# RWKV output scaling from GpSimd to VectorE, with three of the planner's waits made longer

## The chip, the cores and the metric

The kernel runs on one core of one Trainium2 chip. The metric is the device time of one execution in microseconds, the median of several runs. In the profile PE is TensorE (matmuls), PEld its weight loads, DVE is VectorE, ACT is ScalarE, POOL is GpSimd and SP is SyncE, which here issues most of the DMAs. Each engine works through its own queue of instructions in order.

## The reference

A decoder trunk of two layers over one sequence of 1024 tokens, width 1024, all in f32. The first (even) layer runs RWKV-7 time mixing with 16 heads of 64, an S5 state space model and cross-attention to a memory of 256 tokens behind one input projection and one output projection; the second (odd) layer has Mamba-2, latent attention and memory attention in the same layout. The part that matters here is the group norm at the end of the RWKV branch: the outputs `y` of each head and token are centred, scaled and shifted before a bonus is added.

```python
y = seq_major(y).astype(jnp.float32)
mean = jnp.mean(y, -1, keepdims=True)
var = jnp.mean(jnp.square(y - mean), -1, keepdims=True)
y = ((y - mean) * lax.rsqrt(var + RW_GN_EPS)).astype(p.dtype).reshape(b, s, h * n) * ln_w + ln_b
bonus = jnp.sum(r * k * r_k, -1, keepdims=True) * v
return y + bonus.reshape(b, s, h * n)
```

The result is multiplied by a SiLU gate cut from the same input projection.

## The kernel before, in words

Projections are "dense" items: a tile of 128 output columns for two halves of 512 tokens, each half 24 matmuls (8 blocks of the contraction, each in three products of high and low parts), which line 179 issues. They form one long list (`dense`), the lowest in rank: the RWKV projections, then two for the memory's queries, gates, the S5 inputs, the first four S5 gates `zs`, and then an item that waits for `mem`, an event at the start of the S5 stage. Gates are evacuated by ScalarE and by VectorE's line 418.

The RWKV branch is cut into 16 units, each a pair of heads and half of the tokens. For each unit several streams run:

- A (`rw_prep0`) prepares keys and decay. It waits `BK` before the matmuls of the head sums and `HA` before the half products, whose result `ga` ScalarE copies at line 653.
- V (`rw_inv0`) inverts 32x32 triangular blocks: `ga` goes out by DMA (`d_in`), comes back spread over the partitions (`ai`), is worked by 62 small POOL instructions (lines 710 and 712), and goes out and in once more (`d_out`, `xt`). VectorE then transposes small blocks (line 727) for the matmuls of `rw_inv1` (stream I).
- B (`rw_prep1`) makes transposed copies and masks.
- S (`rw_seq`) runs four blocks of 128 tokens one behind the other, and leaves the outputs in a PSUM bank `yps`.
- O (`rw_out`) does the group norm: VectorE sums and centres (lines 841 to 844), ScalarE squares, VectorE sums again (line 848) and finds the reciprocal root with three Newton steps (`rsqrt`, lines 869 to 877) on a 128x8 tile `gmv`; POOL multiplies the 128x512 tile by it (line 850); TensorE transposes the product (line 183); VectorE applies weight and shift, bonus and gate (lines 858 to 862), and SP stores it.

The order of TensorE's instructions is fixed by a planner (`Flow`) when the program is made. It walks through planned microseconds: a stream yields what it waits for (an event, a free PSUM bank, or a number of planned microseconds), and at each step the stream of lowest rank that is ready goes on. A matmul of 512 columns counts 512 / 2400 planned us. A wait in it costs no time on the chip by itself; it decides what TensorE does in between. The tile framework orders the other engines' instructions with a timeline of its own.

The events tie the streams: A of unit n waits for B of unit n-1, B of unit n for A of unit n and S of unit n-2, S of unit n for I and B of unit n. V's due time is made in `stream_a`, from `pool_t[0] = max(pool_t[0], F.now + 10) + HV` and `F.done(("V", n), pool_t[0] + HW - F.now)`, with `HV = 16` and `HW = 14`.

After the last unit the RWKV pools are closed and the S5 stage opens: VectorE and POOL build its parameters, and TensorE begins with transposes of the tile `rn`.

Of the kernel before, what the change touches and what calls it, by code (L numbers as in the profile page):

```python
# [14 lines left out]
A = mybir.AluOpType  # L15
# [109 lines left out]

H = 2.0
HZ = 1.2
HA = 12
HV = 16
S5A = 10  # L130
S5B = 30
HW = 14

S5Q = 12
S5P = 6
MX = 9
MY = 5
ML = 4
BK = 6.5
BL = 1  # L140
S5M = 13
S5Y = 10
# [122 lines left out]
class K:  # L265
# [303 lines left out]
    def rw_prep0(self, st, p, lat, l2, k, wk):  # L569
# [9 lines left out]
        parts = self.pp_parts(sq)  # L579
        yield [BK, ("g", 1)]  # L580
        ps = self.bank("g")
# [44 lines left out]
        ga = wk.tile([P, 4, 2, P], F32, name="ga", bufs=2)  # L626
        yield [HA, ("g", 2)]
        self.half_products(bm, kr, 0, ga)
# [205 lines left out]
    def rw_out(self, p, hh, st, zd, wk):  # L834

        nc, F = self.nc, self.flow
        s = slice(hh * HT, (hh + 1) * HT)
        yp = st["yp"].rearrange("p b (h i) -> p (b h) i", h=2)
        b8 = lambda ap: ap.unsqueeze(2).broadcast_to([P, 8, 64])
        mv = wk.tile([P, 4, 8], F32, name="gmv", bufs=1)  # L840
        nc.vector.tensor_reduce(mv[:, 0], yp, AX.X, A.add)
        nc.vector.tensor_scalar(mv[:, 0], mv[:, 0], 1.0 / 64, None, A.mult)
        y = wk.tile([P, 8, 64], F32, name="ty", bufs=1)
        nc.vector.tensor_tensor(y, yp, b8(mv[:, 0]), A.subtract)
        F.rel("yps", 3.0)
        sq = wk.tile([P, 8, 64], F32, name="sz", bufs=1)
        nc.scalar.square(sq, y)
        nc.vector.tensor_reduce(mv[:, 1], sq, AX.X, A.add)
        self.rsqrt(mv[:, 1], mv[:, 1], mv[:, 2:4], 1.0 / 64, 64e-5)
        nc.gpsimd.tensor_tensor(y, y, b8(mv[:, 1]), A.mult)  # L850
        sz = wk.tile([P, HT], F32, name="sz", bufs=1)
        nc.sync.dma_start(sz, zd[p, :, s])
        yield [10.0, ("g", 1)]
        tp = self.bank("g", (P, 4, P))
        for b in range(4):
            F.transpose(tp[:, b, :], y[:, 2 * b:2 * b + 2].rearrange("p h i -> p (h i)"), self.ident)
        o = wk.tile([P, HT], F32, name="ty", bufs=1)
        nc.vector.tensor_scalar(o, tp.rearrange("p b t -> p (b t)"), self.col("rw_ln_w", p), self.col("rw_ln_b", p),
                                A.mult, A.add)
        F.rel("g", 1.2)  # L860
        nc.vector.tensor_tensor(o, o, st["bon"], A.add)
        nc.vector.scalar_tensor_tensor(o, o, 0.5, sz, A.mult, A.mult)
        self.put_y(p, s, o)
# [49 lines left out]
    def rw_streams(self, cp, wk, rd, zd, npairs=8):  # L913
# [38 lines left out]
        def stream_a():  # L952
            yield "lat"
            lt = latents()
            for n, (p, h) in enumerate(units):
# [8 lines left out]
                pool_t[0] = max(pool_t[0], F.now + 10) + HV  # L964
                F.done(("V", n), pool_t[0] + HW - F.now)

# [1503 lines left out]
```

## Time and profile before

| what | value |
|---|---|
| median of 3 runs | 2760.64 us (2759.63 to 2765.98) |
| the profiled execution's own time | 2757.28 us |
| its span, first to last instruction | 2755.3 us |
| mean granted TensorE clock | 0.954 |
| busy: PE, DVE, ACT, POOL | 2522.3, 1785.2, 1250.2, 804.7 us |

In the rows a line such as `L850 POOL TENSOR_TENSOR ty<-ty,gmv` names the line of the kernel, the engine, the operation and the tiles it writes and reads; `mm` and `g` are PSUM banks. A row of a timeline begins with its start and its length in us, and a bracket at its end tells how long the engine was idle before it and what ended that. A row of stretches gives the stretch, its length, each engine's busy time with the count of its instructions, the granted share of TensorE's clock (1.0 is 2.4 GHz, 0.5 is 1.2 GHz), the share of the DMA engines and GB/s.

### The profile page before, as it was taken

What the parts mean: (1) busy time and instruction counts of PE and PEld (TensorE: products, weight loads), DVE (VectorE), ACT (ScalarE), POOL (GpSimd) and SP (SyncE); (2) the same over time, 40 slices, a digit from 0 to 9 for tenths busy, and PEclk for the clock granted to TensorE, in tenths of its full rate; (3) what the DMA queues carried; (4) which work ended last, traced back from release to release, by engine and by line L of the source; (5) the groups of instructions that cost most, each with busy time, mean ns of one, the idle gap of its engine ahead of it and who ended that gap; (6) DMA issues with size and microseconds to landing.
All of it is one profiled execution on the core that took longest, in us unless ns stands there. A gap on an engine that the chain in (4) does not pass through costs nothing. (4 is left out here: it accounts for less than half of the span.)

```text
span 2755.3 us, 42347 instructions
## 1 busy us (share of the span) xinstructions
PE 2522.3 (92%) x15058; PEld 2036.7 (74%) x15058; DVE 1785.2 (65%) x3366; ACT 1250.2 (45%) x2446; POOL 804.7 (29%) x1507
## 2 busy tenths in 40 slices
PE   7998899999999998888999998988999979998997
PEld 5776677777777776666688776767778768887786
DVE  8756656665755537788656446786743887777532
ACT  7443334443443333545543346435443546655443
POOL 3533554355435403254200111252312020000011
PEclk9999999999999999987999999999999999999999
DMA  4432232333332243355584554142344431113543
GB/s 147 131 100 78 83 94 89 98 89 94 89 100 73 72 133 137 109 151 180 158 280 142 159 183 142 62 108 91 101 144 162 161 117 56 57 50 123 189 133 101
DMA packets 263859, 328.27 MB, mean 119 GB/s; under 512 B 88016, under 2 KB 135248, under 8 KB 263136
## 3 DMA queue, kind: packets, MB, share of 16 engines
q1 hardware_dynamic: 260736, 319.39, 37.6%
q0 software_dynamic: 1280, 4.20, 0.5%
q8 instruction: 119, 1.95, 0.3%
q10 hardware_dynamic: 1632, 1.98, 0.2%
q14 instruction: 92, 0.75, 0.1%
HBM read 232.59 MB, written 92.90 MB: 118 GB/s over the span
## 5 line engine op out<-in xcount | busy, mean ns | idle before, releaser
L405 DVE TENSOR_TENSOR wl<-w,wh 128x512 fp32r<-128x512 f32 (+2 forms) x410 | 287.4, 705 | 282.2 <-ACT wh L404 271.5
L404 ACT CAST wh<-w 128x512 fp32r<-128x512 f32 (+2 forms) x410 | 241.9, 594 | 410.8 <-PE mm L179 259.4
L179 PE MATMUL mm<-xhi,wh 128*128 128x512 f32 x832 | 366.1, 440 | 30.0 <-DVE ev L418 18.5
L179 PE MATMUL mm<-xlo,wh 128*128 128x512 f32 x832 | 341.7, 411 | 4.5 <-DVE xlo L496 2.4
L179 PE MATMUL mm<-xhi,wl 128*128 128x512 f32 x832 | 340.3, 409 | 0.0
L179 PE MATMUL mm<-x1h,wh 128*128 128x512 f32 (+1 forms) x608 | 253.3, 417 | 25.2 <-ACT craw L1818 14.2
L179 PE MATMUL mm<-x1l,wh 128*128 128x512 f32 (+1 forms) x608 | 241.9, 398 | 0.0
L179 PE MATMUL mm<-x1h,wl 128*128 128x512 f32 (+1 forms) x608 | 241.7, 397 | 0.0
L710 POOL TENSOR_TENSOR titmp<-ai,ti 128x60 f32<-128x60 f32 (+24 forms) x496 | 153.1, 309 | 296.5 <-DMA ai<-d_in 259.9
L179 PEld LDWEIGHTS mm<-xhi,wh 128*128 128x128 f32 x832 | 163.9, 197 | 84.6 <-DVE ev L418 20.2
L179 PEld LDWEIGHTS mm<-xhi,wl 128*128 128x128 f32 x832 | 163.8, 197 | 39.7
L179 PEld LDWEIGHTS mm<-xlo,wh 128*128 128x128 f32 x832 | 164.5, 198 | 36.6 <-DVE xlo L474 5.3
L712 POOL TENSOR_TENSOR ti<-ti,titmp 128x60 f32<-128x60 f32 (+24 forms) x496 | 161.3, 325 | 38.2
L179 PEld LDWEIGHTS mm<-x1h,wh 128*128 128x128 f32 (+1 forms) x608 | 117.0, 192 | 59.1 <-ACT craw L1818 17.7
L179 PEld LDWEIGHTS mm<-x1l,wh 128*128 128x128 f32 (+1 forms) x608 | 117.1, 193 | 27.0 <-issue 3.6
L179 PEld LDWEIGHTS mm<-x1h,wl 128*128 128x128 f32 (+1 forms) x608 | 116.6, 192 | 26.8 <-DVE wl L405 0.2
L179 PE MATMUL mm<-yb,wh 128*128 128x512 f32 x320 | 103.6, 405 | 4.3 <-ACT yb L404 4.0
L799 ACT ACTIVATE sn<-s0c,fin 64x64 f32<-64x64 f32 x128 | 44.1, 345 | 104.3 <-DVE s0c L827 57.6
L785 DVE TENSOR_TENSOR gb<-g,m 128x256 f32<-128x256 f32 x128 | 49.4, 417 | 64.3 <-PE g L179 63.8
L1669 POOL TENSOR_TENSOR sq<-sq,sqt 128x512 f32<-128x512 f32 x14 | 18.1, 1289 | 244.9 <-DMA w<-in_w_ev_out 158.8
L418 DVE SCALAR_TENSOR_TENSOR ev<-ev,mm 128x512 f32<-128x512 f32 x72 | 49.0, 681 | 45.5 <-ACT ev L417 45.1
L179 PEld LDWEIGHTS mm<-yb,wh 128*128 128x128 f32 x320 | 61.4, 192 | 20.7 <-ACT yb L404 4.4
(598 smaller groups left out, 6501.7 us busy)
## 6 DMA issues: line engine op xcount, KB each, us to landing
w<-in_w_ev_in SPq DMA_DIRECT2D x106, 256.0 KB
w<-in_w_od_in SPq DMA_DIRECT2D x82, 256.0 KB
w<-in_w_ev_out SPq DMA_DIRECT2D x64, 256.0 KB
w<-in_w_od_out SPq DMA_DIRECT2D x64, 256.0 KB
rd<-ev SPq DMA_DIRECT2D x50, 256.0 KB
spl<-yd SPq DMA_DIRECT2D x40, 256.0 KB
zod<-ev SPq DMA_DIRECT2D x36, 256.0 KB
ai<-d_in SPq DMA_DIRECT2D x16, 512.0 KB
```

Source lines behind the costliest of these rows:

```text
L179: return self._pe(self.nc.tensor.matmul(out, lhsT=lhsT, rhs=rhs, start=start, stop=stop, **kw), math.prod(rhs.shape[1:]), rhs.dtype)
L404: self.nc.scalar.copy(hi, src)
L405: self.nc.vector.tensor_tensor(lo, src, hi.bitcast(F32), A.subtract)
L418: nc.vector.scalar_tensor_tensor(g, g, 1.0, ps, A.add, A.mult)
L710: eng.tensor_tensor(tm, ai[:, s:s + 1, s + 1:32].broadcast_to([P, n, w]), ti[:, 0:n, s:s + 1].broadcast_to([P, n, w]), A.mult)
L712: eng.tensor_tensor(ti[:, 0:n, s + 1:32], ti[:, 0:n, s + 1:32], tm, A.subtract)
L785: nc.vector.tensor_tensor(gb[:, h], pgs[h], self.m2, A.mult)
L799: nc.scalar.mul(sg[hs], sc[hs, hs], g[hs])
L1669: nc.gpsimd.tensor_tensor(self.sq1, self.sq1, t, A.add)
```

## The change

The scaling of line 850 is issued on VectorE instead of POOL, and four numbers of the planner are raised: `HA` from 12 to 13.5, `HW` from 14 to 17, `BK` from 6.5 to 8, and the wait ahead of the transposes of the group norm from 10 to 11 planned us.

```diff
-HA = 12
+HA = 13.5
-HW = 14
+HW = 17
-BK = 6.5
+BK = 8
...
         self.rsqrt(mv[:, 1], mv[:, 1], mv[:, 2:4], 1.0 / 64, 64e-5)
-        nc.gpsimd.tensor_tensor(y, y, b8(mv[:, 1]), A.mult)
+        nc.vector.tensor_tensor(y, y, b8(mv[:, 1]), A.mult)
         sz = wk.tile([P, HT], F32, name="sz", bufs=1)
         nc.sync.dma_start(sz, zd[p, :, s])
-        yield [10.0, ("g", 1)]
+        yield [11.0, ("g", 1)]
```

## Rows read from the trace of the kernel before

**Rows 1.** The page's busy times: us, share of the span, instructions.

```profile
PE 2522.3 (92%) x15058; PEld 2036.7 (74%) x15058; DVE 1785.2 (65%) x3366; ACT 1250.2 (45%) x2446; POOL 804.7 (29%) x1507
```

**Rows 2.** Busy time of each engine in a stretch, the RWKV stage.

```profile
core 0: us, PE busy (x) PEld busy (x) DVE busy (x) ACT busy (x) POOL busy (x), PEclk, DMA share, GB/s
200.00:1056.00 856.00, 799.08 (x6066) 639.68 (x6067) 508.04 (x1123) 330.62 (x708) 362.56 (x981) 0.96 0.31 92
```

**Rows 3.** TensorE's waits, 200 to 1056 us: total, times, longest.

```profile
PE g L183 <- POOL ty L850: 34.5, 13, 6.8
PE g L179 <- DVE xn L727: 10.3, 12, 2.3
```

**Rows 4.** Timeline of TensorE around the output transposes of unit 8.

```profile
661.83 0.44 PE L179 MATMUL g<-s0c,kr 128*128 128x128 f32 x2
669.03 1.12 PE L183 MATMUL g<-ident,ty 128*128 128x128 f32 x4 [6.76 <-POOL ty L850]
```

**Rows 5.** Timeline of POOL in the same stretch.

```profile
667.93 1.04 POOL L850 TENSOR_TENSOR ty<-ty,gmv 128x512 f32<-128x512 f32 x1
...
670.43 0.31 POOL L712 TENSOR_TENSOR ti<-ti,titmp 128x60 f32<-128x60 f32 x1
...
671.22 0.78 POOL L712 TENSOR_TENSOR ti<-ti,titmp 128x76 f32<-128x76 f32 x1
```

**Rows 6.** Timeline of VectorE in the same stretch.

```profile
660.09 0.17 DVE L877 TENSOR_TENSOR gmv<-gmv 128x8 f32<-128x8 f32 x1
...
671.10 0.69 DVE L861 TENSOR_TENSOR ty<-ty,bon 128x512 f32<-128x512 f32 x1
```

**Rows 7.** Sum over the six half-clock stretches behind waits for line 850.

```profile
sum 37.60, PE 27.56 PEld 22.82 DVE 19.56 ACT 0.98 POOL 31.31; mean PE 4.59 PEld 3.80 DVE 3.26 ACT 0.16 POOL 5.22
```

**Rows 8.** Lines 850, 844, 861: ns least/median/most, first and last start.

```profile
L850 POOL TENSOR_TENSOR ty<-ty,gmv x16: 1039/1042/1043, 228.5 to 1047.2; 128x512 f32<-128x512 f32 x16
...
L844 DVE TENSOR_TENSOR ty<-yps,gmv x16: 677/691/693, 211.3 to 1041.1; 128x512 f32<-128x512 f32 x16
...
L861 DVE TENSOR_TENSOR ty<-ty,bon x16: 684/722/803, 232.1 to 1053.5; 128x512 f32<-128x512 f32 x16
```

**Rows 9.** Groups by line, VectorE, 1056 to 1085 us: busy us, mean ns.

```profile
L1306 DVE TENSOR_TENSOR bbr<-bbr,bbt 128x512 f32<-128x512 f32 x1 | 1.8, 1786 | 0.0
```

**Rows 10.** Timelines of ScalarE, POOL, VectorE, TensorE along V of unit 6.

```profile
431.01 1.07 ACT L653 COPY ga<-g 128x512 f32<-128x512 f32 x2
...
445.39 0.24 POOL L710 TENSOR_TENSOR titmp<-ai,ti 128x31 f32<-128x31 f32 x1 [18.00 <-DMA ai<-d_in]
...
470.92 0.22 POOL L712 TENSOR_TENSOR ti<-ti,titmp 128x8 f32<-128x8 f32 x1
...
484.31 1.36 DVE L727 STREAM_TRANSPOSE xn<-xt 32x256 f32<-32x256 f32 x3
...
484.88 0.22 PE L179 MATMUL g<-xn,ga 32*32 32x32 f32 x2 [2.14 <-DVE xn L727]
```

**Rows 11.** Timelines of TensorE and VectorE from the last S to S5.

```profile
1039.75 0.39 PE L179 MATMUL yps<-sa,gr 128*128 128x64 f32 x2
...
1040.26 0.40 PE L179 MATMUL mm<-xlo,wh 128*128 128x512 f32 x1
...
1040.73 0.40 PE L179 MATMUL mm<-xhi,wh 128*128 128x512 f32 x1
...
1046.80 0.17 DVE L877 TENSOR_TENSOR gmv<-gmv 128x8 f32<-128x8 f32 x1
...
1055.30 0.68 DVE L862 SCALAR_TENSOR_TENSOR ty<-ty,sz 128x512 f32<-128x512 f32 x1
...
1084.13 0.72 PE L183 MATMUL g<-ident,rn 128*128 128x128 f32 x4
```

**Rows 12.** Busy time from the last S to the first S5 transposes.

```profile
1040.10:1084.80 44.70, 35.89 (x147) 28.37 (x146) 33.52 (x50) 10.38 (x22) 22.43 (x21) 0.89 0.46 164
```

**Rows 13.** Line 418, the gates' evacuation on VectorE, 1040 to 1100 us.

```profile
L418 DVE SCALAR_TENSOR_TENSOR ev<-ev,mm x7: 674/681/689, 1042.7 to 1095.4; 128x512 f32<-128x512 f32 x7
```

## The prediction

> **What bounds the kernel now.** I read the page's busy shares first: TensorE is busy 2522.3 us of a span of 2755.3 us, 92% [rows 1]. The whole is therefore TensorE's work plus its idle time plus what its work costs at the half clock. The changed lines all lie in the RWKV stage, so the next view is that stage's window. From 200 to 1056 us TensorE is busy 799.1 of 856 us, VectorE 508.0, POOL 362.6, and the granted clock averages 0.96 [rows 2]. The reader should see 57 us of idle TensorE there, and no engine that is full beside it.
>
> The waits of that window say who owns the 57 us. The transposes of the normed output (line 183) waited 34.5 us in 13 waits for POOL's scaling on line 850. The next, 10.3 us in 12 waits, is for VectorE's small transposes of the inverted block (line 727), the end of a chain that I call V below [rows 3].
>
> Unit 8 (counted from 0) shows how. VectorE's last Newton step ends at 660.26 us (660.09 + 0.17) [rows 6]. POOL starts line 850 only at 667.93 us, because it stands in the middle of the 62 small multiplies and subtracts of the next inversion, takes 1.04 us, and is done at 668.97 [rows 5]. TensorE had finished its last matmul at 662.27 and stood 6.76 us, until 669.03 [rows 4]. So POOL's place in its queue is what ends last here, not the length of the multiply.
>
> The waits cost more than themselves. Behind six of the thirteen the granted clock is 0.50 (1.2 of 2.4 GHz) for a while; in those 37.6 us TensorE is busy 27.56 us [rows 7]. At the full clock that work takes half, so 13.8 us are lost, or 0.40 us per us of the 34.5.
>
> **The multiply.** Removed from POOL: 16 instructions of 1042 ns. Added to VectorE: 16 of the same shape. VectorE's lines 844 (PSUM and SBUF in) and 861 (two SBUF inputs) have that shape and take medians of 691 and 722 ns [rows 8]. The upper bound is 1.79 us, which line 1306 took while POOL worked on large tiles [rows 9]. The least of these rows is 0.677 us. I take 0.72, the nearest row: 11.5 us of VectorE over a stage in which it is 59% busy. In unit 8 the product would be ready near 661.0 instead of 668.97, and TensorE reaches the transposes at 662.27. Even at 1.79 us it would be ready at 662.05. In that unit the wait goes whole, and unit 8 is the tightest that I found: its 6.76 us is the longest wait of the thirteen [rows 3]. I take all 34.5 us as gone, and 12 of the 13.8 us of clock. Bounds: the small waits left in each of 13 cases, at most 1.79 - 0.72 = 1.1 us, or 14 us less gain; and no clock gain at all.
>
> A row speaks against this. POOL's subtraction of unit 8 at 671.22 us takes 0.78 us where a neighbour of like shape takes 0.31 [rows 5]; it runs beside line 861, which begins at 671.10 [rows 6]. The Trainium skill, page "SBUF — State Buffer", section "Who interferes with whom", says that a VectorE instruction with two SBUF inputs contends with a GpSimd instruction that reads SBUF, and that the one that issues second is blocked. The trace agrees in kind (0.47 us of stretch). By the rule each moved multiply could hold POOL for all of its length.
> Worked from rows alone: a stretch between 0 and 0.72 us against 1.04 us that leaves the same POOL queue. Either way POOL's chain gets shorter by 0.3 to 1.0 us per unit; the sum does not move.
>
> **The lengthened waits.** TensorE's order is fixed by the planner in planned microseconds, and a planned wait costs no time on the chip: it puts other matmuls in between. So I ask which other work is pulled forward, and what it leaves uncovered.
> The streams form a loop over three units. A (which holds BK and HA) starts V; V is due at least 10 + HV + HW after A; then I, S; the second next B waits for S; the next A waits for that B. One turn holds each constant once: 1.5 + 1.5 + 3 = 6 planned us. Units 0, 3, ... 15 are six turns, so the last S moves back by up to 36 planned us; I take 33, since the first units also wait for projections. At the planner's 512 columns / 2400 = 0.213 us a matmul, that is 155 matmuls; at the chip's spacing of 0.235 us (two between 1040.26 and 1040.73) it is 36 us of projections done earlier [rows 11].
> They exist: behind the last S, which ends at about 1040.1 us, seven half gates are evacuated up to 1100 us [rows 13]. The first was finished at 1040, the other six are 6 x 24 x 0.235 = 34 us. They move in front of that point. That is neutral for TensorE's work, but they cover the change of stage, and there the cover goes.
>
> What is late next there: from the last S at 1040.1 to the S5 transposes at 1084.13, TensorE is busy 35.9 us now, so 8.8 idle [rows 11, 12]. Without the gates it has about 1 us of output transposes and a few matmuls of the memory's keys. The stretch itself shrinks. The Newton steps end at 1047.0, and the transposes' results end on VectorE at 1055.98 [rows 11]. With the product ready at 1047.7, no gates ahead of the transposes, and about 3 us for the transposes and VectorE's three steps behind them (each near the 0.72 of rows 8), that end is near 1051, 5 us earlier. Six gates fewer on VectorE, at 0.68 us each [rows 13], take 4 us more. So about 44.7 - 9 = 36 us with up to 7 busy: 29 idle against 8.8, +20 us. Bounds: +8, if S5's own work starts in the gap, and +30, if none of it shrinks. One more half-clock spell (13.8 / 6) is +2, between 0 and +5.
>
> HW also pays for something. In unit 6, V runs from 432.1 us (two copies of ga) over the DMA (chain starts 445.39 after an 18.0 us wait), POOL (to 471.1) and the DMA again to VectorE's transposes (484.31 to 485.67): 53.6 us, and TensorE waited 2.14 us there [rows 10]. TensorE and V arrive together already. Without the scaling's stall TensorE comes 34.5/16 + 13.8/16 = 3.0 us per unit earlier. HW puts 3 planned us (14 matmuls, 3.3 us) in front, and POOL's chain is 0.3 to 1.0 us shorter. The balance is +0.6 to +1.3 us of slack per unit: the 10.3 us of waits stay about as they are, 0. Bounds: all of it gone with its clock (10.3 x 1.4 = -14), or 0.7 us more in 16 units (+16).
>
> HA gives 1.5 more planned us to the chain of VectorE in front of the half products, BK as much to the split before the head sums. No wait on either appears among the stage's listed ones [rows 3]: nothing saved; what they add is in the six turns. The transposes' 10 to 11 puts 1 us of filling in front of a wait that is gone: 0, and 1 us more idle for the last unit, inside the +20. In SP's queue only the store of the output and the load of its gate come earlier; no DMA is added. If the multiply sat late in VectorE's queue, behind line 858's wait for TensorE, the transposes would wait for it; in program order it stands ahead of that.
>
> **Sum**, against the profiled execution's 2757.28 us (span 2755.3 and 2 around it): -34.5 - 12 + 20 + 2 + 0 = -24.5, so 2732.8. That execution lies 3.4 us below the median of the runs shown, 2760.64; I predict **2736 us**.
>
> **Rivals.**
> (a) V takes the place (no change). The slack per unit is smaller than I think, and TensorE waits longer on line 727. For: TensorE waits for V 12 times in the stage already [rows 3], so there is little slack. Against: HW's 3.3 us are counted for just that. A shortfall of 1.3 us in 13 units costs 13 x 1.3 x 1.4 = 24 us: 2760.
> (b) Slower, the same place and a larger price. The loop is bound by V (DMA, POOL, DMA), and filling placed elsewhere in the loop delays A. Each us of shortfall costs 18 us; from 1.35 us on the change stops paying, from 1.8 us on it is slower by over 0.3%. At 2.5 us: -24.5 + 45 = +21, 2781. For: HW lengthens V's loop while VectorE gains work. Against: POOL's chain gets shorter, not longer.
> (c) More than forecast: with the scaling's stalls gone V's waits go too, and the change of stage costs its lower bound: -34.5 - 13.8 + 8 - 10 = -50, so 2710.
> (d) The scaling still comes late, because VectorE's queue holds it: half of 34.5 and of 12 remains while the +22 is paid: about 0, 2760.
>
> **How the numbers follow.** Forecast (-10 to -40): 0.64. (a) 0.12, (b) 0.09, (c) 0.10, (d) 0.05. Range 2714 to 2758: it holds the forecast, most of (c), and the better halves of (a) and (d). The forecast alone is 2722 to 2750. A measurement of this kernel tells about 0.3%, 8 us. Faster by more: the forecast nearly whole, (c) and a little of (a), 0.76. Same: 0.15. Slower: 0.09.
>
> **What would show it.** Right: line 850 on VectorE at 0.68 to 0.8 us, no wait of line 183 for it, fewer half-clock spells between 200 and 1050 us; the gates of line 418 that now end after 1056 done before the last S; an idle stretch of 25 to 30 us between the last S and the first S5 transposes. Wrong: waits on line 727 above 25 us; or the RWKV stage ends no earlier while the gap behind it opens. If the gap stays under 10 us, the 20 was too high and (c) holds.

## The result, and the profile after

The changed kernel takes 2795.34 us (median of 4 runs, 2789.29 to 2800.22) against 2763.31 us (2759.63 to 2769.24, 4 runs) for the kernel before. The ratio is 1.0108, with an interval of 1.0085 to 1.0131: slower by about 30 us, where 24 us less were forecast. The profiled execution of after took 2789.29 us; it and that of before (2757.28 us) each lie 6 us below their medians, and they differ by 32.0 us as the medians do.

The page's busy times of after, to be read against [rows 1]:

```profile
PE 2529.4 (91%) x15058; PEld 2032.9 (73%) x15058; DVE 1788.3 (64%) x3382; ACT 1245.8 (45%) x2443; POOL 787.4 (28%) x1491
```

The 16 instructions have changed engines and the number of matmuls is the same. TensorE is busy 7 us longer in a span that is 32 us longer.

The span cut at the ends of its stages, after: the stretch, its length, each engine's busy time with its count, the granted clock, the DMA share, GB/s. The cuts are the end of the last S, the first transposes of `rn`, the start of the last pair of copies of `ys` in S5 (line 1463), and the first matmul of the GLU.

```profile
0.00:1062.20 1062.20, 988.44 (x7092) 780.99 (x7092) 660.31 (x1416) 439.51 (x906) 435.51 (x1147) 0.96 0.33 99
1062.20:1098.80 36.60, 9.08 (x40) 7.85 (x41) 28.05 (x41) 3.71 (x10) 20.37 (x19) 0.58 0.32 125
1098.80:1404.00 305.20, 246.72 (x1581) 191.07 (x1579) 223.61 (x326) 148.56 (x306) 110.94 (x97) 0.84 0.46 136
1404.00:1467.50 63.50, 61.49 (x274) 49.24 (x273) 31.68 (x49) 25.63 (x43) 1.24 (x3) 1.00 0.83 271
1467.50:2787.60 1320.10, 1223.70 (x6074) 1003.76 (x6074) 844.70 (x1552) 628.36 (x1178) 219.38 (x227) 0.97 0.38 121
```

The same cuts in the trace of before ([rows 12] is nearly its second line):

```profile
0.00:1040.10 1040.10, 955.10 (x6943) 758.15 (x6944) 645.55 (x1387) 433.25 (x892) 448.02 (x1162) 0.95 0.33 98
1040.10:1084.10 44.00, 35.19 (x143) 27.89 (x143) 32.82 (x50) 9.88 (x22) 21.81 (x20) 0.89 0.46 165
1084.10:1365.50 281.40, 238.50 (x1590) 191.06 (x1589) 226.01 (x326) 149.90 (x308) 114.71 (x95) 0.88 0.50 146
1365.50:1435.70 70.20, 70.20 (x313) 55.73 (x314) 34.71 (x53) 29.75 (x48) 2.19 (x4) 1.00 0.84 277
1435.70:2755.30 1319.60, 1223.36 (x6075) 1003.84 (x6073) 846.12 (x1551) 627.46 (x1178) 217.96 (x227) 0.97 0.38 120
```

| stretch | before | after | change | by the prediction's terms |
|---|---|---|---|---|
| to the last S | 1040.1 | 1062.2 | +22.1 | -34.5 - 12 + 36 = -10.5 |
| change of stage | 44.0 | 36.6 | -7.4 | -9 |
| S5, to the last `ys` | 281.4 | 305.2 | +23.8 | 0 |
| to the GLU | 70.2 | 63.5 | -6.7 | -7 (36 pulled forward less the 29 that lay in the gap) |
| the rest | 1319.6 | 1320.1 | +0.5 | 0 |

The reader should see two lines that miss, the first by 33 us and the third by 24 us. Together they are the whole error of 56.5 us between 2732.8 and 2789.3 (the +2 of the sum for a half-clock spell has no line of its own). The count column shows where the pulled matmuls came from: 149 more up to the last S (7092 against 6943), and against that 103 fewer in the gap, 9 fewer in S5, 39 fewer before the GLU; at the cuts these counts are off by one or two. The first line can be taken apart. TensorE was busy at the half clock for 85.3 us up to the last S in before and for 80.9 us in after. With half of that taken out, its work is 912.5 and 948.0 us: the 149 matmuls cost 35.5 us, near the 36 forecast. Idle time fell by 11 us and the clock gave 2 us, where 46.5 were forecast for both.

TensorE's waits in the RWKV stage of after, 200 to 1056 us (what waited, for what; total, times, longest), against [rows 3]:

```profile
PE g L179 <- ACT rh L807: 16.4, 5, 10.4
PE g L179 <- DVE s0c L827: 12.1, 3, 7.2
PE g L179 <- DVE xn L727: 8.4, 6, 6.0
PE g L179 <- ACT sa L814: 6.5, 3, 3.0
PE mm L179 <- DVE ev L565: 3.7, 1, 3.7
```

Line 850 is gone from the list, and so is its 34.5 us. In its place stand waits for `rh`, `s0c` and `sa` of stream S, and for line 565 (the evacuation of a projection). TensorE's idle time in the same window was 856 - 799.1 = 56.9 us [rows 2] and is now 42.7:

```profile
200.00:1056.00 856.00, 813.30 (x6200) 646.48 (x6200) 515.34 (x1128) 334.20 (x719) 349.30 (x967) 0.96 0.32 94
```

So 14 us of idle time went, not 34.5 (11 up to the last S), and the granted clock is 0.96 as before. What holds VectorE is the other half of the story. Its waits for POOL, 100 to 1062 us, before and then after:

```profile
DVE tg L620 <- POOL tb L587: 17.3, 7, 3.4
...
DVE cc L606 <- POOL ce L599: 9.9, 5, 5.7
```

```profile
DVE cc L606 <- POOL ce L599: 52.5, 13, 8.2
...
DVE tg L620 <- POOL tb L587: 28.2, 7, 7.8
```

27 us of waiting became 81 us. (VectorE's wait for ScalarE at line 418 also grew, from 12.1 to 40.3 us; 19.1 us of that is the case at 1004 us below.) Lines 599 (a memset of 128x4) and 587 (a product) are stream A's own instructions on POOL, in another unit than the one whose inversion runs there. One case, in the timelines of POOL, VectorE and TensorE of after (start, length; the bracket is the idle time before and what ended it):

```profile
486.03 0.22 POOL L712 TENSOR_TENSOR ti<-ti,titmp 128x8 f32<-128x8 f32 x1
491.09 0.40 POOL L705 COPY ti<-t 128x256 f32<-128x256 f32 x1 [4.84 <-DMA d_out<-ti]
491.43 0.10 POOL L599 MEMSET ce<- 128x4 f32 x1
491.49 1.29 POOL L587 TENSOR_TENSOR tb<-tb,tg 128x512 f32<-128x512 f32 x1
```

```profile
484.94 0.66 DVE L418 SCALAR_TENSOR_TENSOR ev<-ev,mm 128x512 f32<-128x512 f32 x1
491.56 1.76 DVE L606 TENSOR_TENSOR cc<-ce 128x516 f32<-128x516 f32 x1 [5.97 <-POOL ce L599]
...
496.78 0.57 DVE L827 SCALAR_TENSOR_TENSOR s0c<-g,fin,sn 64x64 f32<-64x64 f32 x2
```

```profile
497.41 0.49 PE L179 MATMUL g<-s0c,kr 128*128 128x128 f32 x2 [2.93 <-DVE s0c L827]
```

POOL finishes an inversion at 486.25, then its queue stands at the copy of line 705 until the DMA out of `ti` is done, and only behind that comes a memset of 0.10 us. VectorE is idle 5.97 us for it. VectorE then works without a gap over 0.4 us; line 827 of stream S, which has nothing to do with A, comes through the same queue at 496.78, and TensorE waits 2.93 us. In this case 4.84 of the 5.97 us are the copy's wait for the DMA, not the inversion's arithmetic; over the stage that copy stood 71.5 us in 15 times, and 67.5 in before. A second buffer for `ti` was not tried. The longest wait for `rh` has the same form on another engine, without POOL: ScalarE stood 14.59 us for a DMA at the norm of the memory, and the copy of `rh` stood behind it. (The row names the load of a weight; line 1017 itself reads `mraw`, the memory, and in before its wait of 10.8 us is put down to the load of that.) The rows are one of ScalarE and one of TensorE:

```profile
1004.15 0.63 ACT L1017 ACTIVATE macc<-mraw 128x512 f32<-128x512 f32 x1 [14.59 <-DMA w<-in_w_ev_in]
```

```profile
1005.52 1.12 PE L179 MATMUL g<-rh,xt 128*128 128x64 f32 x4 [10.43 <-ACT rh L807]
```

### The profile page after: what moved, and what is told of

Its sections match the earlier page's. It is cut to its first block, busy times and chain, and to the rows that moved or that the text cites. A ratio compares the mean times of both kernels' runs of the same rounds, so it can differ in the third digit from the quotient of the medians.

```text
span 2787.6 us, 42298 instructions
## 1 busy us (share of the span) xinstructions
PE 2529.4 (91%) x15058; PEld 2032.9 (73%) x15058; DVE 1788.3 (64%) x3382; ACT 1245.8 (45%) x2443; POOL 787.4 (28%) x1491
## 5 line engine op out<-in xcount | busy, mean ns | idle before, releaser
L405 DVE TENSOR_TENSOR wl<-w,wh 128x512 fp32r<-128x512 f32 (+2 forms) x410 | 284.3, 697 | 268.0 <-ACT wh L404 260.9
L1822 DVE SCALAR_TENSOR_TENSOR cacc<-craw,hconv,cacc 128x512 f32<-128x512 f32 x72 | 62.5, 868 | 19.7 <-ACT cacc L1820 18.7
```

The costliest lines, as they stand in the source:

```text
L405: self.nc.vector.tensor_tensor(lo, src, hi.bitcast(F32), A.subtract)
L1822: nc.vector.scalar_tensor_tensor(acc, raw[:, k:HT + k], cw(k), acc, A.mult, A.add)
```

## The experiments

Ratios are to the kernel before, run on the same chip, where its median was 2772.3 to 2775.3 us. They are taken over all runs and lie up to 0.4% below the quotient of the two medians; gains in us are worked out from the ratios. Profiles come from several chips, and the kernel before is itself profiled on two below; lengths of the RWKV stage from different chips are not compared finely.

**The change taken apart.** Four planned waits were raised, not three: the wait ahead of the transposes went from 10 to 11. It was not tried by itself. First the multiply alone, with all four waits as before.

```diff
-        nc.gpsimd.tensor_tensor(y, y, b8(mv[:, 1]), A.mult)
+        nc.vector.tensor_tensor(y, y, b8(mv[:, 1]), A.mult)
```

> The multiply on VectorE, all four waits as before. Theory W (the lengthened waits did the harm: they move 35 us of projections ahead of the last S and A's work on POOL under the inversion chain): the 34.5 us wait for line 850 goes, VectorE's wait for POOL's memset of ce (line 599) stays near its 9.9 us of before, and the kernel is 10 to 30 us faster than before, 2735 to 2755. Rival M (taking the stall away is itself what hurts, since TensorE then reaches A while POOL is still in the chain): the wait on line 599 grows to over 30 us here too, and the time is 2760 to 2780.

Measured: 2762.61 us against 2774.5, ratio 0.9943 (0.992 to 0.9966), 16 us less. The gain is what the theory of the waits expected (10 to 30 us); the time itself lies outside its 2735 to 2755 and in the rival's 2760 to 2780, but on this chip the kernel before takes 2774.5 us, so the ratio decides. The wait lists are what the theory of the multiply said. VectorE's and then TensorE's waits of this kernel:

```profile
DVE tg L620 <- POOL tb L587: 43.4, 10, 6.6
DVE cc L606 <- POOL ce L599: 31.6, 13, 5.7
```

```profile
PE g L179 <- ACT rh L807: 22.1, 6, 6.6
...
PE g L179 <- DVE s0c L827: 9.7, 5, 2.9
```

So the multiply alone already moves the stall to lines 599 and 587, 75 us in all, and it is worth 16 us instead of the 46.5 that the prediction gave it. It still gains. Rows of VectorE, ScalarE and TensorE around one wait for `rh` show the way that the stall takes now:

```profile
690.15 0.69 DVE L620 TENSOR_TENSOR tg<-tb,ta 128x512 f32<-128x512 f32 x1 [6.63 <-POOL tb L587]
```

```profile
690.88 0.81 ACT L623 ACTIVATE ta<-ta,oka,cols 128x512 f32<-128x512 f32 x1 [6.86 <-DVE tg L620]
```

```profile
691.91 1.12 PE L179 MATMUL g<-rh,xt 128*128 128x64 f32 x4 [6.61 <-ACT rh L807]
```

VectorE stands at A's line 620 for POOL, ScalarE at A's line 623 for VectorE, and the copy of `rh` (line 807) is next in ScalarE's queue. Four of the six waits for `rh`, 16.5 us, come this way.

Next the waits alone, with line 850 on POOL.

```diff
-HA = 12
+HA = 13.5
-HW = 14
+HW = 17
-BK = 6.5
+BK = 8
...
-        yield [10.0, ("g", 1)]
+        yield [11.0, ("g", 1)]
```

> The four lengthened waits, the multiply left on POOL. Theory W: slower than before by 30 us or more, 2790 to 2825, because the filler moves, the S5 stage loses its order and the wait for line 850 is still there (over 20 us). Rival M: the waits alone only shift filler, and line 850's stall still keeps A behind the chain: 2755 to 2775, with line 599's wait near 10 us.

Measured: 2825.49 us against 2774.5, 1.0181 (1.0148 to 1.0215), 50 us more. The loss of the change is that of the waits; between the multiply alone and both, 1.0108 / 0.9943, they cost 1.7%, some 46 us, where the prediction had +22. The wait for line 850 is still there, as the theory of the waits said; TensorE's wait for it, and VectorE's for A's lines:

```profile
PE g L183 <- POOL ty L850: 45.9, 11, 7.9
```

```profile
DVE cc L606 <- POOL ce L599: 27.3, 6, 9.2
DVE tg L620 <- POOL tb L587: 14.4, 3, 7.8
```

With before, after and the multiply alone this makes a square. With the old waits, moving line 850 raises VectorE's waits for A's two lines from 27.2 to 75.0 us; with the new ones, from 41.7 to 80.7. TensorE's waits for `rh`, `s0c` and `sa` rise with them, from 5.8 to 33.0 us and from 11.7 to 35.0. So the multiply's move brings these waits up with either set of planned waits; in the last of these figures 10.4 us are the case of the norm of the memory, which has nothing to do with POOL.

Two stretches of the kernel with the waits alone, the RWKV stage and S5, and the same of the kernel before in one more profile:

```profile
0.00:1098.30 1098.30, 1003.40 (x7092) 792.91 (x7092) 655.15 (x1401) 440.18 (x906) 452.57 (x1162) 0.94 0.33 96
...
1136.10:1442.40 306.30, 242.43 (x1581) 187.44 (x1579) 224.31 (x326) 148.44 (x306) 109.70 (x95) 0.84 0.46 135
```

> The kernel before, unchanged, for a trace from the same chip as the other experiments. Every theory expects the rows of before: 30 to 38 us of TensorE's waits for line 850, VectorE's wait on line 599 near 10 us, and a last S near 1040 us; only the stretches after the RWKV stage may be a few us longer.

```profile
0.00:1063.40 1063.40, 970.00 (x6943) 769.88 (x6944) 643.39 (x1387) 433.42 (x892) 450.13 (x1162) 0.94 0.33 96
...
1106.70:1390.60 283.90, 240.87 (x1590) 192.81 (x1588) 226.94 (x328) 150.47 (x307) 116.77 (x95) 0.87 0.50 144
```

This execution of the kernel before took 2786.33 us (no edit; one run). Two of its three expectations missed: its waits for line 850 are 45.0 us, not 30 to 38, and its last S ends 23 us later than in the trace of before. That is how far two profiles of one kernel can lie apart here; S5 differs by 2.5 us only. With the waits the RWKV stage is 34.9 us longer than in this one, and 149 matmuls by 0.235 us are 35 us; against the trace of before it is 58 us longer, so the near equality is luck. (This execution lies 14 us above the median on its chip, so the account of the change stays with the trace of before.) That the pulled work went in at its full price, as predicted, rests on the 35.5 us worked out above. But S5 is 22 to 25 us longer than in the two profiles of before, without any work of its own added.

**Where the stall went.** In after, the memset of line 599 is put on VectorE.

```diff
-        nc.gpsimd.memset(ce[:, :, 0:1], 0.0)
+        nc.vector.memset(ce[:, :, 0:1], 0.0)
```

> The changed kernel with A's memset of one column of ce (line 599) on VectorE instead of POOL. Theory Q (the new waits of TensorE in the RWKV stage are VectorE's queue held by that memset, which stands behind the 62 small POOL instructions of another unit's inversion): VectorE's 52.5 us of waiting on line 599 goes, the last S ends 10 to 20 us earlier than 1062, and the time is 2775 to 2785. Rival (VectorE then simply waits at line 620 for POOL's product tb of line 587, in the same place): line 620's 28.2 us grows to over 50 and the time stays 2790 to 2800.

Measured: 2800.37 us, 1.0087 (1.0057 to 1.0117), no better than after. The rival is right (its range ended at 2800); VectorE's wait list of this kernel has only the next instruction of A behind the same queue:

```profile
DVE tg L620 <- POOL tb L587: 72.8, 13, 10.1
```

So both must leave together. This is done on the multiply alone, with the waits of before.

```diff
-        nc.gpsimd.tensor_tensor(d2, d2, kh, A.mult)
+        nc.vector.tensor_tensor(d2, d2, kh, A.mult)
...
-        nc.gpsimd.memset(ce[:, :, 0:1], 0.0)
+        nc.vector.memset(ce[:, :, 0:1], 0.0)
```

> The multiply on VectorE with the waits as before, and A's two POOL instructions that VectorE waits for (line 599, the memset of a column of ce, and line 587, the product tb) on VectorE as well. Theory Q (the stall of line 850 came back as VectorE's queue, held by these two behind the inversion's 62 small instructions): VectorE's 75 us of waits on lines 599 and 587 go, TensorE's waits for rh and s0c (32 us) fall below 12, and the kernel is 1.0 to 1.8% faster than before (ratio 0.982 to 0.990; the multiply alone had 0.994). Rival (the loop is held by V's own latency, so the waits move on to line 727): line 727's wait grows to over 25 us and the ratio stays 0.992 to 0.998.

Measured: 2744.64 us against 2775.29, 0.9888 (0.9859 to 0.9917). This is the fastest of all, faster than both kernels, and the total expected by the theory of the queue. Its waits for lines 599 and 587 are gone, and so are TensorE's for `s0c`. Its limit on `rh` was missed: TensorE and VectorE still wait so:

```profile
PE g L179 <- ACT rh L807: 25.8, 5, 8.5
```

```profile
DVE rk L667 <- POOL km L664: 33.0, 7, 8.1
```

A third instruction of the same kind, line 664, has come up on POOL. ScalarE's row before one of the five waits for `rh` shows it:

```profile
637.42 0.62 ACT L404 CAST ce<-rk 128x512 fp32r<-128x512 f32 x1 [6.16 <-DVE rk L667]
```

Three of the five (15.3 us) are of this form: ScalarE stands at line 404 for VectorE's line 667, which stands for POOL's line 664. One (8.5 us) is the norm of the memory again, where ScalarE stood 12.2 us for a DMA, and one (2.0 us) follows the load of a weight. TensorE's idle time up to the last S, behind its first matmul, is 64.8 us, only 1.9 less than with the multiply alone; it is busy at the half clock for 93.8 us against 105.3, but these are profiles from two chips. So the ratio shows that the two lines gain, and the profile does not show the gain as idle time. And one wait ahead of the stretch listed above has grown: up to 141 us ScalarE stood 17.2 us for POOL's line 614, against 7.7 with the multiply alone, and TensorE waited 11.9 us behind it, against 2.4.

I moved line 664 and two small ones (lines 613 and 614) as well.

```diff
-        nc.gpsimd.tensor_copy(fin[:, 4:8], e[:, :, P])
-        nc.gpsimd.tensor_tensor(fin[:, 8:11], fin[:, 4:7], fin[:, 1:4], A.mult)
+        nc.vector.tensor_copy(fin[:, 4:8], e[:, :, P])
+        nc.vector.tensor_tensor(fin[:, 8:11], fin[:, 4:7], fin[:, 1:4], A.mult)
...
-        nc.gpsimd.tensor_tensor(km, b3(k2), em, A.mult)
+        nc.vector.tensor_tensor(km, b3(k2), em, A.mult)
```

> The fastest so far (multiply, lines 599 and 587 on VectorE, waits as before) with lines 613, 614 and 664 on VectorE too, so that POOL keeps the inversion and one product of A. Theory Q carried on (what is left of TensorE's waits for rh, 25.8 us, is ScalarE and VectorE held by fin and km behind the inversion): the waits for rh fall under 12 us and the ratio to before is 0.978 to 0.986. Rival (the rest is V's own latency and VectorE's load): rh's waits move to line 727 or to the evacuations, ratio 0.987 to 0.993.

Measured: 2759.58 us against 2772.3, 0.9945 (0.9925 to 0.9965): worse than the two lines alone, and outside the ranges of both theories. The waits for `rh` (21.1 us) neither fell under 12 us nor moved to line 727, which costs 10.1 us between 200 and 1056 us against 9.8 with the two lines. Line 664 now waits on VectorE itself, for line 624 on POOL (VectorE's list):

```profile
DVE km L664 <- POOL rk L624: 35.1, 6, 12.9
```

Where it loses is not shown. In the one profile its last S ends at 1015.1 us, 11 us before that of the two lines, and S5 takes 291.6 us against 279.8; the two are from different chips, and the profiled execution of this kernel is the fastest of its six.

**What the waits cost in S5.** In after, the third of the S5 gates, and with it all that stands behind it in the list, is held until the RWKV stage is over, so that it fills S5 again.

```diff
+        zs[2].wait = "rwend"
...
         F.run(self.rw_streams(cp, wk, rd, zr))
+        F.done("rwend")
```

> The changed kernel, but the third of the S5 gates (and all items behind it) waits for the end of the RWKV stage, as it stood in the order before. Theory S (the S5 stage lost 21 us because its projections and the loads for the output projection run ahead of S5's own chain): the stretch from the first S5 transposes to the last S5 output falls from 305 us to 281 to 288, and the time is 2768 to 2782. Rival (that stretch is disturbed by chance, or the tail of the RWKV stage then stands idle by as much as is won): 2788 to 2800.

Measured: 2786.01 us, 1.0031 (1.001 to 1.0051), 0.77% or 21 us less than after. Time and stretch miss the expected ranges narrowly (2782 and 288 us). S5 of this kernel:

```profile
1105.40:1393.90 288.50, 242.27 (x1587) 193.86 (x1586) 221.81 (x325) 154.43 (x312) 105.18 (x92) 0.85 0.48 142
```

So S5's length follows, in these kernels, the projections that are left for it. Counted in the traces, S5 holds 396 matmuls of input and memory projections in before, 348 in after and 393 with the gates held; the output projection, which comes behind them in the list, has 108, 135 and 108 there. So the total in S5 hardly changes (1590, 1581, 1587), but more of it has to wait for loads and splits first. The lengths: 279.8 to 291.6 us in the five with the waits of before (284.3 with the multiply alone, 279.8 and 291.6 with A's lines moved), 305.2 to 307.3 in the three with all of them and the gates early, 288.4 and 288.5 in the two with the gates held. The number alone is not a rule: the last kernel below has 462 such matmuls in S5 and takes 293.4 us. What TensorE waits for there in after, beside [rows 13], whose gates now all end before the last S:

```profile
PE mm L179 <- ACT yh L404: 9.5, 3, 5.6
PE g L179 <- ACT mpt L1172: 8.4, 1, 8.4
PE mm L179 <- DVE yl L405: 6.7, 4, 4.5
```

In before these three are 0.8, 0.9 and 2.9 us. The gates that stood here are done, and the output projection of the RWKV branch's outputs (`yh`, `yl`) comes up so early that TensorE waits for their split into high and low parts (lines 404 and 405). To see whether its place alone is the cost, I let it be released 20 planned us later in after.

```diff
-                F.done(("ya", 0), 2.0)
+                F.done(("ya", 0), 22.0)
```

> The changed kernel, with the planner told that the first loads for the output projection (event ya, half 0) are due 22 planned us after their issue instead of 2. Theory Y (of the 21 us lost in the S5 stage most is TensorE waiting for those loads and their splits, yh and yl, because the projection now comes too early in S5): the waits for yh and yl (16 us) fall under 5, the stretch from the first S5 transposes to the last S5 output falls from 305 us to under 293, ratio 1.001 to 1.006. Rival (the loss is the gates missing between S5's own steps, whatever stands in their place): the stretch stays over 298 and the ratio 1.008 to 1.013.

Measured: 2797.87 us, 1.0079 (1.0051 to 1.0107). The stretch misses its expectation narrowly, and the ratio is near the rival's. Waits for `yh` and `yl` are gone from TensorE's list, but another has come (S5's stretch and TensorE's wait):

```profile
1111.30:1404.50 293.20, 230.73 (x1554) 181.39 (x1552) 223.61 (x323) 144.67 (x302) 109.67 (x96) 0.86 0.48 137
```

```profile
PE g L179 <- DMA mq<-qd: 18.6, 1, 18.6
```

Neither reading is clean here; putting that projection later only shows the next hole. Holding the gates is what fills it.

**Do two causes explain the whole?** After, with the gates held and A's two lines on VectorE (the edits above together):

> The changed kernel with the third S5 gate held to the end of the RWKV stage, and lines 599 and 587 on VectorE. If the two causes found (S5's order, POOL's queue in A) are the whole of the harm beside the filler itself, the ratio falls from 1.003 (gates held alone) by what the two lines give the kernel with the old waits, 0.4 to 1.2%: 0.991 to 0.999. If the longer waits hurt in a further way (V and the loop's own pace), it stays 1.000 to 1.004.

Measured: 2760.78 us against 2775.29, 0.993 (0.9906 to 0.9955), inside the range expected. The two edits take 1.8% off the change, from 1.0108, and all four of its waits still stand. The two causes are not quite the whole: with the old values of the waits the two lines give 0.9888, so the waits still cost 0.4% and are not worth having.

**Which of the waits.** On the multiply alone, first `HW`, then `HA` and `BK`.

```diff
-HW = 14
+HW = 17
```

> The multiply on VectorE and HW at 17; HA, BK and the transposes' wait as before. Theory L (harm goes with the planned us that a turn of the loop gains, whichever constant holds them: 3 of 6 here): about 75 more 512-column matmuls before the last S than the 2155 of before, against 149 with all, and half of the harm: ratio 1.000 to 1.005. Rival (HA and BK alone do the harm, since they move A's POOL work; HW only gives V time): ratio 0.990 to 0.996, with line 599's wait under 35 us.

```diff
-HA = 12
+HA = 13.5
-BK = 6.5
+BK = 8
```

> The multiply on VectorE, HA at 13.5 and BK at 8; HW and the transposes' wait as before. Theory L: the same 75 matmuls and the same ratio as with HW alone, 1.000 to 1.005. Rival (HA and BK do the harm): 1.006 to 1.012, with VectorE's wait on line 599 near the 52 us of the changed kernel.

Measured: `HW` 2773.7 us, 0.9989 (0.9973 to 1.0005), so +0.5% on the multiply's 0.9943, between the two expectations; `HA` and `BK` 2801.41 us, 1.0088 (1.0063 to 1.0113), +1.5%. The equal shares of the first theory are out. The total of the second is what the rival expected, but not by the way it gave: the waits for line 599 are 28.0 us there, not near 52. The projections' matmuls before the last S are 2155 with the multiply alone, 2254 with `HW` and 2281 with the other two. In S5 both pay alike (298.9 and 300.4 us). The difference lies in the RWKV stage, `HW` first:

```profile
0.00:1041.10 1041.10, 968.48 (x7042) 765.73 (x7043) 659.28 (x1410) 438.70 (x900) 443.03 (x1147) 0.96 0.34 100
```

```profile
0.00:1062.80 1062.80, 995.89 (x7069) 788.88 (x7070) 655.11 (x1413) 437.13 (x903) 439.30 (x1147) 0.94 0.33 98
```

27 matmuls more are 6 us, and TensorE is busy 27 us longer, at a clock of 0.94 against 0.96. The mean clock of every run says the same (0.936 to 0.945 with `HA` and `BK`, 0.948 to 0.955 with `HW`). It is not the sum of idle time: from these rows TensorE is idle 72.6 us with `HW` and 66.9 with the other two. Why `HA` and `BK` lower the clock was not found.

Last, the other direction: the fastest kernel with `HW` at 11.

```diff
-HW = 14
+HW = 11
```

> The fastest so far (multiply, lines 599 and 587 on VectorE, BK, HA and the transposes' wait as before) with HW at 11 instead of 14, the change's own step of 3 taken the other way. Theory L (a planned us less in the loop leaves filler for the change of stage and for S5, where it covers more): some 70 to 100 matmuls fewer before the last S than 2155, the stretch from the first S5 transposes to the last S5 output not longer than 284 us, ratio 0.978 to 0.986. Rival (V's own latency of over 50 us is the bound, and TensorE now reaches line 727 first): line 727's waits grow from 14 to over 40 us and the ratio is 0.989 to 1.000.

Measured: 2812.99 us against 2773.58, 1.0105 (1.0044 to 1.0166): 2.2% worse than with 14. The rival is right on the waits, and the loss is more than it said (0.989 to 1.000). TensorE's waits and the RWKV stage:

```profile
PE g L179 <- DVE xn L727: 46.2, 28, 6.2
```

```profile
0.00:1078.10 1078.10, 990.52 (x6877) 788.53 (x6878) 653.74 (x1430) 431.61 (x887) 419.25 (x1115) 0.89 0.32 93
```

With 66 matmuls fewer than at 14 this stage is 52 us longer: the waits on line 727 grew from 14.1 to 46.2 us, TensorE is idle 16 us longer in all, and the granted clock is 0.89 against 0.94.

## Why the prediction was wrong

**Right.** Line 850 takes a median of 691 ns on VectorE (0.68 to 0.8 was forecast) and TensorE no longer waits for it, but for 6.9 us in the last unit. The projections' matmuls before the last S rose by 149 (155 forecast). TensorE's idle time in the change of stage rose from 8.8 to 27.5 us, +18.7 (forecast +20), and the stretch shrank by 7.4 (forecast 9). Line 727 cost no more than before (8.4 us against 10.3); rival (a), that V takes the place, is out, and so is (d), that the scaling comes late in VectorE's queue. Rival (b) had the sign but not the mechanism: waits on line 727 are 8.4 us, not 25.

**POOL's time.** The forecast that the chain on POOL gets no longer holds: POOL's busy time fell by 17.3 us, from 804.7 [rows 1] to 787.4, and 16 instructions of 1042 ns are 16.7. The Trainium skill, page "SBUF — State Buffer", section "Who interferes with whom", allows each moved multiply to hold POOL for its length; the totals of this trace show no such loss. Single cases of the two engines in each other's way are there: line 606 above takes 1.76 us beside POOL's line 587, against its median of 0.70.

**Wrong, first step: "I take all 34.5 us as gone, and 12 of the 13.8 us of clock."** The stall left line 850 and came back. I had looked at what waits for POOL's scaling and found that POOL's place in its queue ends last. The inversion that blocked the scaling is still there, and so are A's own instructions behind it. TensorE's stall had covered a good part of them: with either set of planned waits, VectorE's waits for lines 599 and 587 rise by 39 to 48 us when line 850 leaves POOL. That the stall did it by giving the two lines time, while TensorE stood at line 183, is my reading. Now VectorE stands at 606 and 620 with S's small steps behind it, and ScalarE behind VectorE. Idle time up to the last S fell from 78.4 to 67.4 us, by 11, and the time that TensorE is busy at the half clock from 85.3 to 80.9. That is 13 us of gain, half of 4.4 being what the clock gave, for a forecast of 46.5. Against the other profile of before, a slower execution, the same sum would give 38 us; what does not hang on one profile is that the multiply alone gained 16 us by its ratio. The multiply alone (0.9943), the memset alone (no gain) and both of A's lines together (0.9888) show this. The largest wait that the two lines leave is for `rh`, 25.8 us, of which 15.3 come from line 664, the next on POOL; moving that one too did not win it. And 10.4 of the 16.4 us for `rh` in after are the norm of the memory, not POOL. The size of the stall was itself uncertain: 34.5 us in one profile of before, 45.0 in the other.

**Wrong, second step: the projections pulled forward priced only where they uncover the change of stage.** The +20 there was right. But S5 is a chain of small steps, which the last input projections had filled, and with 48 of their matmuls gone it took 23.8 us more, 15.6 of them idle. Holding the gates back gave 21 us of after's loss again. The sum had no term for it; the third line of the table is where it should have stood. The +2 for one more half-clock spell did not come in the change of stage: TensorE was busy at the half clock for 5.3 us there before and 5.7 after. In S5, which had no term, that time rose from 59.4 to 70.5 us, and the granted clock went from 0.88 to 0.84.

**Open.** Why `HA` and `BK` cost three times what `HW` does for a like number of matmuls (126 and 99 more); why moving three more lines off POOL lost time; and how much of POOL's hold is the copy of line 705 waiting for its DMA.

## What to carry to other kernels

Before one instruction is taken out of a queue that a long serial chain blocks, list every other instruction of other streams behind that chain: the next of them is the new stall, through whichever engine waits for it. Moving more of them is to be tried one by one: here two more gained and three more beside them lost. Work that is pulled forward as filler is taken from somewhere: price every later stage that it filled, not only the first gap. And take such a change apart first: here one line gained 0.6%, four planned waits lost 1.7%, and two further lines beside the first brought the gain to 1.1%.

## What was not expected of the hardware

More can be lost with the clock than with the waits it goes with: 28 waits on line 727, 46.2 us in pieces of at most 6.2, went with a granted clock of 0.89 over the first 1078 us, against 0.94 over 1026 us in the same kernel with the longer wait. That is 213 us of TensorE's busy time at 1.2 GHz against 94, some 60 us lost, for 16 us more of idle time. It is one pair of kernels on two chips, and what about the waits does it was not tried; with `HA` and `BK` against `HW` the clock was lower with less idle time. And the same kernel, before, had 85 us at that level in one profile and 119 in another, so that 17 us of its RWKV stage are the clock's alone.
